# A decoder layer's output projection: the residual added by accumulating transfers, the second norm in rows of its own

## The chip, the cores and the metric

The kernel runs on one core of a Trainium2 chip. The metric is the device time of one execution in microseconds (us), lower is better. The time before is the median of three runs. The profile is that of one further execution, whose own time stands in the table below beside its span.

## The reference

One layer of a decoder with 1024 tokens of 1024 numbers, all in float32. What the change touches is the middle of it:

```
m = concat([rmsnorm(a, attn_group_norm), rmsnorm(c, conv_group_norm)])
x = x + rmsnorm(m @ w_out, mix_post_norm)          # x1
h = rmsnorm(x, ffn_pre_norm)
f = (silu(h @ w_gate) * (h @ w_up)) @ w_down
x = x + rmsnorm(f, ffn_post_norm)
x = x + sigmoid(x @ w_ple_gate) * rmsnorm(p @ w_ple_proj, ple_norm)
```

Ahead of it stand the first norm, the combined input projection, latent attention with 8 heads (`a`) and a gated short convolution (`c`).

## The kernel before, in words

The layer is computed stage after stage: input projection and convolution, attention by heads, output projection, gate and up projections of the feed-forward part, down projection, and the last gate. Every product is split in two: a number is written as a high and a low part (`split`, lines 209 and 210: a cast on ScalarE, a difference on VectorE), and three matmuls take the place of one. The feed-forward products are arranged as seven products of half-size blocks in place of eight (`factor` builds the weight side, `product` does the 12 matmuls of one, lines 1192 to 1195).

Memory is handed out by the program itself. `mf(n)` takes n units of 512 float32 columns from an arena of 30 units, and `free` gives them back; among free places the one that has been free longest is taken. A second argument limits the place: `ML` is units 0 to 22, `MG` 18 to 22, `MW` 0 to 8. Whoever writes into a place waits for the last reader of what was there.

The order of the work on each engine is not quite that of the program. A planner (the Tile scheduler) goes through the program with durations of its own and puts first on an engine what it believes to be ready; each engine and each DMA queue then runs its list strictly in order. All transfers of this stage are issued by SyncE (SP).

The output projection works through eight row tiles t of 128 tokens. The attention half is multiplied here (`wo_half`, 24 matmuls); the convolution half was multiplied earlier, and its rows wait in DRAM as `y_d`. One pass of the loop at the end of the printed code does, for different tiles:

- `wo_a(t)`: 24 matmuls; VectorE adds them, scaled, to the row y loaded from `y_d` (line 1071); `row_norm(t, 0)` takes the mean square on ScalarE (line 230), adds epsilon on VectorE (line 226) and raises to the power -0.5 on GpSimd (line 227).
- `wo_x1(t - 1)`: VectorE multiplies y by the norm and a gain, in place (line 1077), adds the row of x (line 1079), SyncE stores the sum as x1 (line 1081), and `row_norm(t - 1, 1)` takes the second mean square.
- `load_x(t)`: SyncE loads the next row of x (line 1059).
- `wo_n(t - 2)`: VectorE multiplies y by the second norm and gain, in place (line 1086).
- `h2_turn(t - 3)`: TensorE transposes the row (line 1106), ScalarE and VectorE copy it out. The first four tiles are split into `B11` and `B21` and stored raw in `hr_d` (line 1116); the last four go into `tr`, `b12` and `b22` below.
- `load_y(t + 2)` (line 1055) and, near the end, `raw_load` of raw gate and up weights (line 1148).

In the passes after the last tile the first four products of the feed-forward stage run; they need `B11` and `B21` of the first four tiles only. The next eight products (`fp` 1 and 2) need the same and raw weights. Everything after needs sums over all eight tiles (line 1303): `t2` and the splits `T1` to `T4`, of `b12`, `b22` and of `hr_d` read back.

Of the kernel before, what the change touches and what calls it, by code (L numbers as in the profile page):

```python
# [12 lines left out]
ALU = mybir.AluOpType  # L13
AX = mybir.AxisListType

P = 128
# [29 lines left out]
T = S // P  # L46
# [53 lines left out]
def free(*bufs):  # L100
    for b in bufs:
        m = b.arena
        m.clock += 1
        for i in range(b.lo, b.lo + b.n):
            assert m.live[i]
            m.live[i] = False
            m.freed[i] = m.clock
# [28 lines left out]
def hybrid_layer(ctx: ExitStack, tc: tile.TileContext, x, x_t, p_t, cols_in, positions,  # L136
# [3 lines left out]
    act, dve, pe, pool, sp = nc.scalar, nc.vector, nc.tensor, nc.gpsimd, nc.sync  # L140

    x, out = x[0], out[0]
# [10 lines left out]
    mf = Arena(big.tile([P, FU * U], F32, name="mem_f"), FU)  # L153
# [21 lines left out]
    ML, MG, MW = ((0, 22),), ((18, 22),), ((0, 8),)  # L175
# [24 lines left out]
    def cols(n):  # L200
        lo = small_at[0]
        small_at[0] += n
        assert small_at[0] <= 128
        return small[:, lo : lo + n]

    def split(h, l, src, gain=None, eng=None):

        if gain is None:
            act.copy(h, src)  # L209
            (eng or dve).tensor_tensor(l, src, h.bitcast(F32), op=ALU.subtract)  # L210
        else:
            act.mul(h, src, gain)
            dve.scalar_tensor_tensor(l, src, gain, h.bitcast(F32), op0=ALU.mult,
                                     op1=ALU.subtract)
# [20 lines left out]
    def bank3(ap, k):  # L235
        return ap.rearrange("p (k c) -> p k c", k=k)
# [330 lines left out]
    for step in START.split():  # L567
        op, t = step[0], int(step[1:] or 0)
# [412 lines left out]
    ss_y = cols(2 * T)  # L981
# [63 lines left out]
    g_mix, g_ffn = mf(2, MG), mf(2, MG)  # L1045
# [2 lines left out]

    rows_y, rows_x = {}, {}

    def load_y(t):
        rows_y[t] = mf(2, ML)
        sp.dma_start(rows_y[t].a, y_d[t * P : (t + 1) * P, :])

    def load_x(t):
        rows_x[t] = mf(2, ML)
        sp.dma_start(rows_x[t].a, x[t * P : (t + 1) * P, :])

    def row_norm(t, i):
        r = ss_y[:, 2 * t + i : 2 * t + i + 1]
        junk = mr(2, BJ)
        mean_sq(junk.a, rows_y[t].a, D, r)
        free(junk)
        rstd_of(r)

    def wo_a(t):
        y = rows_y[t].a
        ids, b = wo_half(t, mTa, 0)  # L1070
        dve.scalar_tensor_tensor(y, b, ss_a[:, t : t + 1], y, op0=ALU.mult, op1=ALU.add)
        ps.put(ids)
        row_norm(t, 0)

    def wo_x1(t):
        y, xr = rows_y[t].a, rows_x.pop(t)
        dve.scalar_tensor_tensor(y, y, ss_y[:, 2 * t : 2 * t + 1], g_mix.a, op0=ALU.mult,
                                 op1=ALU.mult)
        dve.tensor_tensor(y, y, xr.a, op=ALU.add)
        free(xr)  # L1080
        sp.dma_start(x1_d[t * P : (t + 1) * P, :], y)
        row_norm(t, 1)

    def wo_n(t):
        y = rows_y[t].a
        dve.scalar_tensor_tensor(y, y, ss_y[:, 2 * t + 1 : 2 * t + 2], g_ffn.a, op0=ALU.mult,
                                 op1=ALU.mult)

# [2 lines left out]
    def four(b):  # L1093
        return b.a.rearrange("p (k c) -> p k c", k=4)

    def h2_turn(t):
        src = rows_y.pop(t)
        o = slice(t % 4 * P, (t % 4 + 1) * P)
        first = t < T // 2
        if first:  # L1100
            raw = mf(2, ML)
        for q in range(2):
            ids, b = ps.get()
            for j in range(4):
                k = 4 * q + j
                pe.transpose(b[:, j * P : (j + 1) * P], src.a[:, k * P : (k + 1) * P], ident[:])
            if first:
                act.copy(raw.a[:, q * U : (q + 1) * U], b)
            else:
                act.copy(four(tr[q])[:, :, o], bank3(b, 4))  # L1110
            if first or q:
                h, l = tf["B" + "12"[q] + "12"[not first]]
                split(four(h)[:, :, o], four(l)[:, :, o], bank3(b, 4))
            ps.put(ids)
        if first:
            sp.dma_start(hr_d[:, :, o], raw.a.rearrange("p (k c) -> p k c", k=KD))
            free(raw)
        free(src)
# [12 lines left out]
    def pair(n, where):  # L1131
        return mr(n, where), mr(n, where)
# [11 lines left out]
    def raw_load(fp, i, where=None):  # L1144

        for m, w in enumerate((w_gate, w_up)):
            raws[fp, m, i] = r = mf(2, where)
            sp.dma_start(r.a, w[2 * fp + i])

    def factor(fp, m, p):  # L1150
        eng = pool if fp else dve
        a = raws[fp, m, 0].a
        a11, a12 = a[:, 0:U], a[:, U:]
        if p == 1:
            src = a11
        elif p == 2:
            src = a12
        else:
            b = raws[fp, m, 1].a
            a21, a22 = b[:, 0:U], b[:, U:]  # L1160
            if p == 6:
                eng.tensor_tensor(a21, a21, a22, op=ALU.add)
                eng.tensor_tensor(a11, a21, a11, op=ALU.subtract)
                src = a11
            elif p == 5:
                src = a21
            elif p == 7:
                eng.tensor_tensor(a21, a22, a11, op=ALU.subtract)
                src = a21
            elif p == 3:  # L1170
                eng.tensor_tensor(a12, a12, a11, op=ALU.subtract)
                src = a12
            else:
                src = a22
        h, l = wp[fp, m, p] = pair(1, RR)
        split(h.a, l.a, src)
        if p == ORDER[-1]:
            free(raws.pop((fp, m, 0)), raws.pop((fp, m, 1)))
# [75 lines left out]
    for t in range(T + 3):  # L1254
        if t < T:
            wo_a(t)
        elif t == T:
            for d in (mTa, wo):
                for h, l in d.values():
                    free(h, l)  # L1260
            for i in head[:2]:
                product(*i)
        elif t == T + 1:
            for i in head[2:]:
                product(*i)
        if 1 <= t <= T:
            wo_x1(t - 1)
        if t < T:
            load_x(t)
        if 2 <= t <= T + 1:  # L1270
            wo_n(t - 2)
        if t == T + 1:
            free(g_mix, g_ffn)
            t2 = mf(4, MG)
            tf["T1"], tf["T4"] = pair(4, BT), pair(4, BT)
            b11, b21 = tf["T1"][1].a.bitcast(F32), tf["T4"][1].a.bitcast(F32)
            sp.dma_start(b11.rearrange("p (k c) -> p k c", k=4), hr_d[:, 0:4, :])
            sp.dma_start(b21.rearrange("p (k c) -> p k c", k=4), hr_d[:, 4:8, :])
        if t >= 3:
            h2_turn(t - 3)  # L1280
        if t + 2 < T:
            load_y(t + 2)
        if t == T - 1:
            raw_load(0, 1, ML)
        if t == T:
            raw_load(1, 0, ML)
        if t == T // 2:
            for i in head:
                factor(*i)
    b12, b22 = tr[0], tr[1]  # L1290

    def both(f, fp, p):
# [239 lines left out]
    for i in range(n2):  # L1532
# [17 lines left out]
        if j in tail:  # L1550
            f, t = tail[j]
# [66 lines left out]
```

## Time and profile before

| | |
|---|---|
| median of three runs | 1226.24 us (1225.47 to 1227.34) |
| the profiled execution's own time | 1227.49 us |
| its span, first to last instruction | 1225.4 us |
| mean granted TensorE clock | 0.99 |
| busy: TensorE, VectorE, ScalarE, GpSimd | 98%, 66%, 48%, 41% |
| output projection's tiles and the change's reach | about 438 to 531 us of the span |

In the rows of the profile, PE is TensorE (PEld its weight loads), DVE VectorE, ACT ScalarE, POOL GpSimd, SP SyncE; L1071 is line 1071 of the code. A row of the timeline gives start, duration, engine, line, operation, what it writes and reads, and in brackets how long the engine was idle before and what ended that. A row of the waits gives who waited, for whom, the total, how often, and the longest.

### The profile page before, as it was taken

The page shows a single profiled execution, that of the slowest core. Times are in us where ns is not written, and L with a number is a line of the kernel's source. Part 1 is how long each engine was busy: PE and PEld are TensorE (multiplying, and loading weights), DVE is VectorE, ACT ScalarE, POOL GpSimd, SP SyncE. Part 2 cuts the span into 40 slices and gives each one's busy share as a digit, 9 for nine tenths or more (in the row PEclk, how much of TensorE's full clock was granted, in tenths as well). Part 3 has the DMA queues.
Part 4 walks back from the last instruction along what each step waited for, and adds up shares of the span by engine and source line. Part 5 has one row for each costly group of instructions (what it writes and reads, how often), then busy time and mean ns, then how long its engine had stood idle before and what let it go on. Part 6 is the DMA issues. An engine that isn't in the chain of part 4 may idle for free.

```text
span 1225.4 us, 16706 instructions
## 1 busy us (share of the span) xinstructions
PE 1201.5 (98%) x5918; PEld 1012.2 (83%) x5918; DVE 810.6 (66%) x1173; ACT 587.3 (48%) x1079; POOL 503.8 (41%) x392
## 2 busy tenths in 40 slices
PE   8999999999999999789999999999999999999998
PEld 6998888889999888678788888888888888888886
DVE  6676346478867758785657665565556677758775
ACT  7543333267766736543433333333345546545652
POOL 4433534226554311025888646674634102202321
PEclk8999999999999999889999999999999999999999
DMA  8712553994561667524465445543566576654342
GB/s 267 258 39 104 184 202 133 278 365 90 135 161 44 232 223 252 203 104 143 161 229 197 140 144 190 178 157 118 209 209 200 184 242 230 233 172 164 120 136 79
DMA packets 89821, 217.77 MB, mean 178 GB/s; under 512 B 9030, under 2 KB 18026, under 8 KB 88426
## 3 DMA queue, kind: packets, MB, share of 16 engines
q1 hardware_dynamic: 89392, 216.17, 53.4%
q8 instruction: 46, 0.75, 0.3%
q10 hardware_dynamic: 346, 0.54, 0.2%
q14 instruction: 37, 0.30, 0.1%
HBM read 145.38 MB, written 71.04 MB: 177 GB/s over the span
## 4 chain that ended last, share of the span: by engine, by line
PE 80%; DVE 6%; DMA 5%; issue 3%; ACT 3%; POOL 2%; ACTq 0%; POOLq 0%; DVEq 0%; SPq 0%
PE banks L1192 10%; PE banks L1195 10%; PE banks L1194 10%; PE banks L220 7%; PE banks L222 7%; PE banks L221 7%; PE banks L1391 6%; PE banks L1390 6%; PE banks L1389 6%; PE banks L894 2%; DVE mem_r L210 2%; PE banks L1498 1%; PE banks L1501 1%; PE banks L1500 1%; PE banks L865 1%
## 5 line engine op out<-in xcount | busy, mean ns | idle before, releaser
L210 DVE TENSOR_TENSOR mem_r<-mem_f,mem_r 128x512 fp32r<-128x512 f32 (+1 forms) x404 | 374.4, 958 | 206.4 <-ACT mem_r L209 194.1
L209 ACT CAST mem_r<-mem_f 128x512 fp32r<-128x512 f32 (+2 forms) x407 | 258.4, 666 | 410.6 <-PE banks L1194 128.7
L1192 PE MATMUL banks<-mem_r 128*128 128x512 f32 x616 | 242.0, 393 | 4.5 <-ACT mem_r L209 3.4
L1194 PE MATMUL banks<-mem_r 128*128 128x512 f32 x616 | 241.6, 392 | 0.0
L1195 PE MATMUL banks<-mem_r 128*128 128x512 f32 x616 | 240.8, 392 | 0.1
L220 PE MATMUL banks<-mem_r 128*128 128x512 f32 (+2 forms) x536 | 196.3, 371 | 2.4 <-ACT mem_r L209 1.7
L221 PE MATMUL banks<-mem_r 128*128 128x512 f32 (+2 forms) x536 | 196.4, 368 | 1.3 <-POOL mem_r L210 1.2
L222 PE MATMUL banks<-mem_r 128*128 128x512 f32 (+2 forms) x536 | 196.0, 368 | 0.0
L1192 PEld LDWEIGHTS banks<-mem_r 128*128 128x128 f32 x616 | 116.5, 189 | 30.7 <-ACT mem_r L209 5.0
L1195 PEld LDWEIGHTS banks<-mem_r 128*128 128x128 f32 x616 | 116.7, 189 | 25.7 <-DVE mem_r L210 1.1
L1194 PEld LDWEIGHTS banks<-mem_r 128*128 128x128 f32 x616 | 116.8, 190 | 24.3 <-DVE mem_r L210 0.2
L1391 PE MATMUL banks<-mem_r 128*128 128x512 f32 x308 | 119.8, 389 | 0.0
L1390 PE MATMUL banks<-mem_r 128*128 128x512 f32 x308 | 119.8, 389 | 0.0
L1389 PE MATMUL banks<-mem_r 128*128 128x512 f32 x308 | 119.8, 390 | 0.0
L220 PEld LDWEIGHTS banks<-mem_r 128*128 128x128 f32 x536 | 101.2, 190 | 19.1 <-ACT mem_r L209 2.8
L221 PEld LDWEIGHTS banks<-mem_r 128*128 128x128 f32 x536 | 101.6, 190 | 17.4 <-POOL mem_r L210 1.4
L222 PEld LDWEIGHTS banks<-mem_r 128*128 128x128 f32 x536 | 101.5, 189 | 16.1
L879 POOL TENSOR_TENSOR mem_f<-mem_f,stats 128x640 f32<-128x640 f32 (+5 forms) x64 | 73.4, 1161 | 92.0 <-DVE stats L878 49.4
L227 POOL TENSOR_TENSOR small<-small,mhalf 128x1 f32<-128x1 f32 (+2 forms) x46 | 37.6, 821 | 177.5 <-DVE small L226 177.0
L1210 DVE TENSOR_TENSOR mem_f<-banks,mem_f 128x512 f32<-128x512 f32 x66 | 45.2, 686 | 55.9 <-PE banks L1195 55.8
L210 DVE TENSOR_TENSOR mem_r<-banks,mem_r 128x512 fp32r<-128x512 f32 (+3 forms) x118 | 69.3, 612 | 12.9 <-ACT mem_r L209 12.3
L1390 PEld LDWEIGHTS banks<-mem_r 128*128 128x128 f32 x308 | 57.8, 188 | 12.0
(197 smaller groups left out, 1890.0 us busy)
## 6 DMA issues: line engine op xcount, KB each, us to landing
sc_d<-mem_f SPq DMA_DIRECT2D x77, 256.0 KB, 3.5
mem_f<-sc_d SPq DMA_DIRECT2D x77, 256.0 KB, 3.0
mem_f<-in_w_gate_dram SPq DMA_DIRECT2D x22, 512.0 KB, 5.2
mem_f<-in_w_up_dram SPq DMA_DIRECT2D x22, 512.0 KB, 5.1
mem_f<-in_w_down_dram SPq DMA_DIRECT2D x22, 512.0 KB, 4.5
wc_d<-mem_f SPq DMA_DIRECT2D x22, 512.0 KB, 2.7
mem_f<-wc_d SPq DMA_DIRECT2D x44, 256.0 KB, 3.1
mem_f<-in_w_down_dram SPq DMA_DIRECT2D x33, 256.0 KB, 3.4
```

The costliest lines, as they stand in the source:

```text
L209: act.copy(h, src)
L210: (eng or dve).tensor_tensor(l, src, h.bitcast(F32), op=ALU.subtract)
L220: pe.matmul(o, wh, vh, start=i == 0, stop=False)
L221: pe.matmul(o, wh, vl, start=False, stop=False)
L222: pe.matmul(o, wl, vh, start=False, stop=i == n - 1)
L879: pool.tensor_tensor(pt.a[:, 0:n], pt.a[:, 0:n], sm.to_broadcast([P, n]), op=ALU.mult)
L1192: pe.matmul(b, wh.a[:, c], th[:, k], start=first and k == 0, stop=False, skip_group_check=True)
L1194: pe.matmul(b, wh.a[:, c], tl[:, k], start=False, stop=False, skip_group_check=True)
L1195: pe.matmul(b, wl.a[:, c], th[:, k], start=False, stop=k == 3, skip_group_check=True)
L1389: pe.matmul(b, ah.a[:, c], bh.a, start=first, stop=False, skip_group_check=True)
L1390: pe.matmul(b, ah.a[:, c], bl.a, start=False, stop=False, skip_group_check=True)
L1391: pe.matmul(b, al.a[:, c], bh.a, start=False, stop=last, skip_group_check=True)
```

## The change

The row of x is no longer loaded into a buffer and added by VectorE. A transfer on the GpSimd queue reads it from DRAM and adds it to y in memory (`accum_op`). The x1 store and the second mean square follow that transfer. The second norm writes into new rows (`rows_n`), and y is freed there. y is loaded one tile later than before in program order, the two raw weight loads of the loop may use units 0 to 18 only, the two gains are freed at separate points, and `t2` is taken after the loop.

```
-    rows_y, rows_x = {}, {}
+    rows_y = {}
...
-    def load_x(t):
-        rows_x[t] = mf(2, ML)
-        sp.dma_start(rows_x[t].a, x[t * P : (t + 1) * P, :])
...
     def wo_x1(t):
-        y, xr = rows_y[t].a, rows_x.pop(t)
+        y = rows_y[t].a
         dve.scalar_tensor_tensor(y, y, ss_y[:, 2 * t : 2 * t + 1], g_mix.a, op0=ALU.mult,
                                  op1=ALU.mult)
-        dve.tensor_tensor(y, y, xr.a, op=ALU.add)
-        free(xr)
+        pool.dma_start(y, x[t * P : (t + 1) * P, :], accum_op=ALU.add)
         sp.dma_start(x1_d[t * P : (t + 1) * P, :], y)
         row_norm(t, 1)
 
+    rows_n = {}
+
     def wo_n(t):
-        y = rows_y[t].a
-        dve.scalar_tensor_tensor(y, y, ss_y[:, 2 * t + 1 : 2 * t + 2], g_ffn.a, op0=ALU.mult,
-                                 op1=ALU.mult)
+        y = rows_y.pop(t)
+        rows_n[t] = mf(2, ML)
+        dve.scalar_tensor_tensor(rows_n[t].a, y.a, ss_y[:, 2 * t + 1 : 2 * t + 2], g_ffn.a,
+                                 op0=ALU.mult, op1=ALU.mult)
+        free(y)
...
     def h2_turn(t):
-        src = rows_y.pop(t)
+        src = rows_n.pop(t)
...
-        if t < T:
-            load_x(t)
+        if t == T:
+            free(g_mix)
         if 2 <= t <= T + 1:
             wo_n(t - 2)
         if t == T + 1:
-            free(g_mix, g_ffn)
-            t2 = mf(4, MG)
+            free(g_ffn)
...
-        if t + 2 < T:
-            load_y(t + 2)
+        if 1 <= t < T - 1:
+            load_y(t + 1)
         if t == T - 1:
-            raw_load(0, 1, ML)
+            raw_load(0, 1, ((0, 18),))
         if t == T:
-            raw_load(1, 0, ML)
+            raw_load(1, 0, ((0, 18),))
...
+    t2 = mf(4, MG)
```

## The prediction

> **What bounds the kernel now.** I read the page first, then the busy time by stretches around the output projection, what TensorE waited for there, and last the order of VectorE, ScalarE and SyncE in the same stretch.
>
> ```profile
> span 1225.4 us, 16706 instructions
> PE 1201.5 (98%) x5918; PEld 1012.2 (83%) x5918; DVE 810.6 (66%) x1173; ACT 587.3 (48%) x1079; POOL 503.8 (41%) x392
> ```
>
> TensorE is busy for 98% of the span, so whatever another engine saves counts only where TensorE stands still. The changed stage is one such place (columns: stretch, its length, busy time and count of PE, PEld, DVE, ACT, POOL, then the granted clock, the DMA share, GB/s):
>
> ```profile
> 444.00:484.00 40.00, 40.00 (x195) 33.47 (x194) 33.12 (x41) 21.02 (x40) 7.90 (x11) 1.00 0.72 237
> 484.00:498.00 14.00, 13.75 (x67) 10.82 (x65) 12.99 (x20) 9.57 (x17) 2.48 (x4) 1.00 0.74 245
> 498.00:531.00 33.00, 22.45 (x81) 17.58 (x82) 26.68 (x27) 16.25 (x24) 0.93 (x1) 0.74 0.43 156
> 531.00:560.00 29.00, 28.94 (x126) 23.28 (x125) 20.96 (x20) 11.97 (x21) 12.43 (x9) 1.00 0.37 127
> ```
>
> TensorE runs through 444 to 498 without a gap, loses 33.00 - 22.45 = 10.55 us idle between 498 and 531, and is full again after that. In the same stretch the granted clock is 0.74, so of the 22.45 busy microseconds 22.45 x 0.26 = 5.8 are slow clock. At most 10.55 + 5.8 = 16.4 us can be won here. The two gaps and what ended them:
>
> ```profile
> PE banks L1106 <- issue: 7.3, 1, 7.3
> PE banks L1192 <- ACT mem_r L209: 3.4, 2, 3.1
> 484.45 0.73 PE L1192 MATMUL banks<-mem_r 128*128 128x512 f32 x2
> 505.09 1.94 PE L1106 MATMUL banks<-ident,mem_f 128*128 128x128 f32 x8 [7.34 <-issue]
> 507.37 0.79 PE L1192 MATMUL banks<-mem_r 128*128 128x512 f32 x1 [0.34 <-ACT mem_r L209]
> 525.31 0.79 PE L1192 MATMUL banks<-mem_r 128*128 128x512 f32 x1 [3.09 <-ACT mem_r L209]
> 525.90 0.63 PE L1194 MATMUL banks<-mem_r 128*128 128x512 f32 x1
> 526.33 0.63 PE L1195 MATMUL banks<-mem_r 128*128 128x512 f32 x1
> 531.57 0.40 PE L1194 MATMUL banks<-mem_r 128*128 128x512 f32 x1
> 531.80 0.40 PE L1195 MATMUL banks<-mem_r 128*128 128x512 f32 x1
> ```
>
> The projection's last matmul is over at 484.45, where the first products of the next stage begin. The first gap ends with row tile 6's transposes (L1106), the second with a split of late weights (L209). After a gap matmuls start 0.43 us apart (525.90 to 526.33) and only about six microseconds later 0.23 apart (531.57 to 531.80).
>
> Why the transposes are late is VectorE's order:
>
> ```profile
> 448.43 1.28 DVE L1071 SCALAR_TENSOR_TENSOR mem_f<-banks,small,mem_f 128x1024 f32<-128x1024 f32 x1
> 451.76 1.29 DVE L1077 SCALAR_TENSOR_TENSOR mem_f<-mem_f,small 128x1024 f32<-128x1024 f32 x1 [0.67 <-POOL small L227]
> 479.83 1.28 DVE L1071 SCALAR_TENSOR_TENSOR mem_f<-banks,small,mem_f 128x1024 f32<-128x1024 f32 x1 [0.48 <-DMA mem_f<-y_d]
> 490.61 1.27 DVE L1071 SCALAR_TENSOR_TENSOR mem_f<-banks,small,mem_f 128x1024 f32<-128x1024 f32 x1
> 496.71 1.22 DVE L1079 TENSOR_TENSOR mem_f<-mem_f 128x1024 f32<-128x1024 f32 x1
> 503.71 1.28 DVE L1086 SCALAR_TENSOR_TENSOR mem_f<-mem_f,small 128x1024 f32<-128x1024 f32 x1 [4.39 <-DMA x_d<-mem_f]
> 508.56 1.28 DVE L1086 SCALAR_TENSOR_TENSOR mem_f<-mem_f,small 128x1024 f32<-128x1024 f32 x1
> 511.78 1.03 PE L1106 MATMUL banks<-ident,mem_f 128*128 128x128 f32 x8
> ```
>
> Row 6's second norm (503.71) writes in place over y, so it waited 4.39 us for the x1 store that reads y. Row 7's norm follows at 508.56, its transposes end at 512.8. Row 7 was late before that: TensorE had it ready at 484.4, but its sum with y began at 490.61. SyncE tells why:
>
> ```profile
> 486.03 0.32 SPq L1055 DMA_DIRECT2D mem_f<-y_d  x1
> 493.09 0.33 SPq L1059 DMA_DIRECT2D mem_f<-in_x_dram  x1
> 498.33 0.49 SPq L1148 DMA_DIRECT2D mem_f<-in_w_gate_dram  x1
> 521.18 0.33 SPq L1148 DMA_DIRECT2D mem_f<-in_w_up_dram  x1
> SPq L1055 <- DMA hr_d<-mem_f: 10.6, 3, 5.8
> SPq L1059 <- DMA hr_d<-mem_f: 6.1, 1, 6.1
> ```
>
> The seven two-unit slots that 22 units leave beside four for raw weights and four for gains hold y, x and the transposed rows. Three y loads and one x load waited for an hr_d store to leave a slot (10.6 and 6.1 us), row 7's y and x among them, and SyncE stood behind them.
>
> **The change part by part.** *The sums go.* Eight L1079 sums of 1.22 leave VectorE. Off the path that is nothing; on it, in 484 to 498, where VectorE is busy 12.99 of 14.00, it lets row 7's steps start when their inputs are there.
>
> *The accumulate comes.* Eight transfers on the GpSimd queue, each behind its L1077 and ahead of the x1 store and the second mean square. No row shows one. The nearest are plain 512 KB transfers, median issue to landing, the first two lines from 444 to 484, the others from 484 to 510:
>
> ```profile
> x_d<-mem_f SPq DMA_DIRECT2D x6, 512.0 KB, 2.9
> mem_f<-in_x_dram SPq DMA_DIRECT2D x4, 512.0 KB, 4.8
> x_d<-mem_f SPq DMA_DIRECT2D x2, 512.0 KB, 9.4
> mem_f<-in_w_up_dram SPq DMA_DIRECT2D x2, 512.0 KB, 10.8
> 451.17 0.56 POOL L227 TENSOR_TENSOR small<-small,mhalf 128x1 f32<-128x1 f32 x1 [4.14 <-DVE small L226]
> 453.19 1.52 POOL L227 TENSOR_TENSOR small<-small,mhalf 128x1 f32<-128x1 f32 x1 [1.46 <-DVE small L226]
> ```
>
> So L, from the end of L1077 to landing, lies between 2.9 and 10.8; it cannot be below zero, since a transfer must follow the norm. I take 6: x's own load, 4.8, plus 1.2 for GpSimd's issue, between the 0.56 and 1.52 of its other instructions. The same row reaches memory as before, so the total of bytes loaded stays.
>
> A rule of the Trainium skill speaks against it. Here DMA runs at 0.72 to 0.74 of its time over 444 to 498, at some 240 GB/s. The Trainium skill's "Collectives: The Full Stack", section "The bandwidth ceiling: the fold count and why AG ≠ RS ≠ AR", says that an add inside the DMA path needs two source reads and halves the rate. No run here shows it yet; by it, L would be nearer 10, row 7 four microseconds later, the gain some 4 us smaller, 1220.6 in place of 1216.6.
>
> *Row 7's chain.* From the start of L1071 to L1077 an unhindered row takes 451.76 - 448.43 = 3.33 (square, add, power between). New chain: sum at 484.5, L1077 at 487.8, done 489.1, landed 489.1 + L, second norm's square, add and power 3.33 - 1.28 = 2.05, L1086 1.28, transposes about 1.0: end at 493.4 + L, so 499.4 with L = 6 and 504.2 with 10.8, against 512.8. The x1 store is off this path, since L1086 writes rows of its own (same 1.28).
>
> *Queues.* On GpSimd the issue waits for L1077; behind it stands the next row's power, some 1.5 us at worst, and VectorE waits for that. It is covered by a row's TensorE time, 24 matmuls x 0.23 + 1.0 = 6.5 us. On SyncE the x1 store now waits for the accumulate, and y(t+1), which the program now asks for one row later, may stand behind it. Its slot is free rows earlier, so the planner can issue it first. If not, a row may start only 4.61 (L1071 to the end of L1077) + L + 0.3 issue + 4.8 load = 15.7 after the one two before it, in place of 13: 1.35 us a row, seven rows, 9.5 us, and the tail stands at 508.9, still before 512.8. The eight x issues leave SyncE.
>
> *Slots and weights.* Tracing the allocator by hand through the old loop gives the waits above: y(5), y(6), y(7) and x(7) in the slots of hr_d stores, and the gate weights (1,0) in x(7)'s, issued at 498.33, just after x(7)'s sum ended at 497.93. The same tracing for the new loop puts y(4) to y(7) in slots that the second norm or the transposes gave up rows before, gate (1,0) in y(6)'s and up (1,0) in the fifth norm row's. y(6)'s slot is free when row 6's second norm has read it and its x1 store has landed: 479.83 + 4.61 + 6 = 490.4 for the accumulate, and 2.9 to 9.4 for the store, so 493.3 to 499.8 (the norm is done at 493.8). With 4.8 to 10.8 for the load and 1.3 for split and cast, gate (1,0) is usable between 499.9 and 511.9, middle 506. Up (2,0) still takes b12's slot, as it did at 521.18, 8.4 after the last transposes; it moves with them to 507.8.
>
> *The sum.* TensorE has its first four products until 498, as before, then two tiles of transposes (2 us), and if the planner puts the up weights first, 2.7 us of their products (12 matmuls x 0.23): until 502. Waiting until 506 leaves one gap of 4 us. The slow clock behind it costs what it cost at 525, 14 matmuls x 0.2 = 2.8. Left over is 6.8 of 16.4; the gain is 9.6 us. All else (the gains freed earlier, t2 after the loop) issues no instruction and is taken at nothing; it has the full TensorE after 531 to hide in. The profiled execution took 1227.49 (span 1225.4 and 2.1 around it), 1.25 over the median of 1226.24: 1217.9 for it, 1216.6 for the median.
>
> On the re-warming the row differs from a page: from 525.31 the slow matmuls last until about 531. The Trainium skill's "TensorE: Matmul & The Clock Gate", section "What's actually happening", gives 3.4 us of sustained work for it; by that the gap would cost 1.7, not 2.8, and the time be 1215.5.
>
> **The rivals.** *No change: the weights were the wait.* At 507.37 the first product came 0.34 us after the transposes, released by a split, so weights loaded from 498.33 were about as late. If gate (1,0) is again issued near 498 and lands as slowly, only the 1.94 us of transposes move into the gap: 1224.3. For it: DMA is crowded with hr_d, x1 and weights at the tail. Against it: y(6)'s slot comes free up to 5 us earlier, and half of the weights do not wait for it.
>
> *Slower: ScalarE waits for the transfer with the next row behind it.* ScalarE works in order. If a row's second square stands ahead of the next row's first, the row period is L1077 1.28 + L + two squares 2.5 + add and power 0.8 = L + 4.6 against TensorE's 6.5. Over seven rows the tail ends at 493.4 + L + 7 (L - 1.9) = 480.1 + 8L: later than 512.8 from L = 4.1 on. At 4.8 it is 518.5, 5.7 later, 1231.9; at 6 it is 528.1, 15.3 later, 1241.5. Against it:
>
> ```profile
> 449.75 1.06 ACT L230 ACTIVATE mem_r<-mem_f 128x1024 fp32r<-128x1024 f32 x1 [3.54 <-DVE mem_f L1071]
> 450.88 1.06 ACT L230 ACTIVATE mem_r<-mem_f 128x1024 fp32r<-128x1024 f32 x1
> ```
>
> The square at 449.75 is row 1's first (it follows the L1071 of 448.43); row 0's second comes behind it, at 450.88. With two rows in flight the period is (L + 4.6) / 2, harmless until L = 8.4. For it: the planner orders by its own durations, and none of its guesses for an accumulate is visible here.
>
> *The accumulate is far dearer.* With L above 493.4 + L = 512.8, 19.4 us, the tail would be as late as now; no transfer of this size in the rows took that long. It counts as part of the slower case.
>
> **How the numbers follow.** The forecast has 0.62, no change 0.15, slower 0.23. Its own bounds are 1209.8 (all 16.4 won) and 1222.5 (gate weights at 511.9 in place of 506: 5.9 less gained). The range 1209.8 to 1231.9 takes in the no-change case and the near end of the slower one; what it leaves out is the far half of that case, 0.12, and little below. A measurement of this kernel tells about 0.2%, 2.5 us, from no change. Faster by more than that: 0.62 + 0.02 of the no-change case, 0.64; within: 0.13; slower: 0.23.
>
> **What would show it.** Right: no x loads on SyncE, eight accumulates landing in about 6 us, L1071 of row 7 within a microsecond or two of 484.5, its transposes over near 500, no wait of L1086 for an x1 store, TensorE's idle time after 498 at about 4 us, at one place, behind weights. Wrong: second squares that hold up ScalarE row after row, y loads behind x1 stores, idle time of TensorE before 498, or accumulates of 10 us and more.

## The result, and the profile after

The changed kernel takes 1234.65 us, the median of five executions, against 1226.24 before (1225.47 to 1227.48). Four of the five lie between 1231.76 and 1236.88; the fifth, of 3653.29, and one of e8 below, of 2434.99, are left out of the ratios. The ratio is 1.0063 with a 95% interval of 1.0043 to 1.0083: slower by about 8 us, where 9.6 us less was forecast. The profiled execution took 1234.65 as well, with a span of 1232.9, 7.5 over the span before.

The lines of the page that answer to those of before:

```profile
span 1232.9 us, 16712 instructions
PE 1201.0 (97%) x5918; PEld 1011.2 (82%) x5918; DVE 804.9 (65%) x1165; ACT 587.8 (48%) x1079; POOL 512.9 (42%) x400
```

Eight sums have left VectorE and eight issues have come to GpSimd. TensorE's busy time is the same, so the time went where TensorE stands still or runs slowly. Busy time by stretches, in the prediction's columns:

```profile
444.00:484.00 40.00, 37.47 (x178) 30.24 (x178) 22.78 (x30) 15.84 (x29) 10.39 (x16) 1.00 0.77 196
484.00:498.00 14.00, 10.39 (x38) 7.93 (x37) 11.09 (x16) 9.65 (x20) 3.60 (x5) 0.76 0.96 253
498.00:531.00 33.00, 23.53 (x107) 19.25 (x106) 22.37 (x26) 18.20 (x28) 3.50 (x4) 0.84 0.64 204
531.00:560.00 29.00, 27.06 (x113) 20.45 (x111) 26.87 (x24) 14.97 (x22) 11.37 (x7) 1.00 0.31 110
```

Idle time is 2.53 + 3.61 + 9.47 + 1.94 = 17.55 us, against 0.25 + 10.55 + 0.06 = 10.86 before. Slow clock costs 10.39 x 0.24 + 23.53 x 0.16 = 6.3, against 5.8. Together 23.8 against 16.7: 7.2 of the 7.5 us lie in these stretches. The 10.55 us after 498 have become 9.47, so little was won there; new are 6.1 us of idle time before 498, where TensorE stood for only 0.25.

The waits that grew are those for the new transfer (columns: waiter, releaser, sum of us, times, longest):

```profile
ACT mem_r L230 <- DMA mem_f<-in_x_dram: 16.1, 5, 6.0
PE banks L1192 <- ACT mem_r L209: 10.3, 3, 8.7
SPq L1077 <- DMA mem_f<-in_x_dram: 31.3, 6, 13.0
ACT mem_f L1108 <- DMA hr_d<-mem_f: 5.8, 3, 2.4
```

ScalarE stands five times, 16.1 us in all, in front of a second mean square (L230) whose row is still being accumulated: rows 0, 1, 2, 6 and 7. In rows 3 to 5 the landing is over before the square's turn comes; there the copies of a transposed row (L1108) stand ahead of it, and they wait three times, 5.8 us in all, for a store of `hr_d` to leave their slot. The accumulates themselves, by the view of their line, are about as long as forecast in the median:

```profile
L1076 POOL DMA_DIRECT2D mem_f<-in_x_dram x8: 884/886/1068, 447.7 to 505.7; - x8
DMA to landing us min/median/max: 5.4/5.8/10.0
```

How a wait on one engine reaches TensorE is seen at rows 2 and 4, on the timelines of VectorE, GpSimd, SyncE, ScalarE, VectorE and TensorE, in this order (start, duration, instruction, idle time before it and its releaser):

```profile
458.17 1.28 DVE L1074 SCALAR_TENSOR_TENSOR mem_f<-mem_f,small 128x1024 f32<-128x1024 f32 x1 [0.66 <-POOL small L227]
...
460.01 0.89 POOL L1076 DMA_DIRECT2D mem_f<-in_x_dram  x1 [1.88 <-DVE small L226]
...
470.37 0.59 SPq L1116 DMA_DIRECT2D hr_d<-mem_f  x1
...
470.07 1.06 ACT L230 ACTIVATE mem_r<-mem_f 128x1024 fp32r<-128x1024 f32 x1 [5.96 <-DMA mem_f<-in_x_dram]
...
471.25 0.15 DVE L226 TENSOR_SCALAR small<-small 128x1 f32<-128x1 f32 x1 [5.24 <-ACT mem_r L230]
471.33 1.28 DVE L1067 SCALAR_TENSOR_TENSOR mem_f<-banks,small,mem_f 128x1024 f32<-128x1024 f32 x1
...
472.67 0.50 PE L220 MATMUL banks<-mem_r 128*128 128x512 f32 x1 [1.73 <-DVE mem_f L1067]
```

Row 2's accumulate is issued at 460.01 and lands at 470.0. ScalarE waits 5.96 for it, VectorE waits 5.24 for ScalarE, and right behind stands row 4's sum (L1067), which empties TensorE's banks: TensorE waits 1.73 for that. All three engines work in order, so one late landing holds row 4, whose own inputs were there. It also holds SyncE: row 2's x1 store goes out at 470.00, and only behind it, at 470.37, the first `hr_d` store, for which the later copies then wait. From L1074 of row 2 to that of row 4 (474.70, below) 16.5 us pass.

While row 2's accumulate was on its way the DMA engines had hardly a free moment. The same ten microseconds in the changed kernel, then in e1 below, which has the same instructions without the add:

```profile
460.00:470.00 10.00, 10.00 (x53) 8.48 (x52) 4.76 (x6) 3.09 (x6) 2.91 (x4) 1.00 0.99 247
460.00:470.00 10.00, 10.00 (x51) 8.40 (x50) 6.99 (x10) 4.65 (x11) 2.79 (x5) 1.00 0.87 291
```

They were busy for 0.99 of the time and moved less, 247 GB/s against 291.

The same loop from row 4 to row 6, where the landing is no longer what the square waits for, on VectorE, GpSimd, SyncE, ScalarE and VectorE again:

```profile
474.70 1.28 DVE L1074 SCALAR_TENSOR_TENSOR mem_f<-mem_f,small 128x1024 f32<-128x1024 f32 x1 [0.66 <-POOL small L227]
...
476.28 0.88 POOL L1076 DMA_DIRECT2D mem_f<-in_x_dram  x1 [1.62 <-DVE mem_f L1074]
...
481.95 0.32 SPq L1077 DMA_DIRECT2D x_d<-mem_f  x1
...
483.55 0.59 ACT L1108 COPY mem_f<-banks 128x512 f32<-128x512 f32 x1 [2.45 <-DMA hr_d<-mem_f]
...
485.47 1.09 ACT L230 ACTIVATE mem_r<-mem_f 128x1024 fp32r<-128x1024 f32 x1
...
486.76 1.28 DVE L1067 SCALAR_TENSOR_TENSOR mem_f<-banks,small,mem_f 128x1024 f32<-128x1024 f32 x1
490.07 1.28 DVE L1074 SCALAR_TENSOR_TENSOR mem_f<-mem_f,small 128x1024 f32<-128x1024 f32 x1 [0.66 <-POOL small L227]
```

From L1074 of row 4 to its issue 1.58; to the landing, marked by the x1 store that waited for it, 5.67; to the second square 3.52, because a transposed row's copies stand ahead on ScalarE and waited 2.45 for a store to leave their slot; to row 6's sum 1.29; to row 6's L1074 3.31. That is 15.37 us for two rows, 7.7 a row, where TensorE needs 6.5. In e1, without the add, the same loop takes 15.8 (467.60 to 483.38): what the changed kernel loses against e1 it has lost by row 4.

The tail, on the same timelines; the landing is that of the load at 502.50 alone:

```profile
494.87 1.28 DVE L1067 SCALAR_TENSOR_TENSOR mem_f<-banks,small,mem_f 128x1024 f32<-128x1024 f32 x1
...
503.19 0.69 DVE L1162 TENSOR_TENSOR mem_f<-mem_f 128x512 f32<-128x512 f32 x1 [4.58 <-DMA mem_f<-in_w_gate_dram]
503.86 1.27 DVE L1074 SCALAR_TENSOR_TENSOR mem_f<-mem_f,small 128x1024 f32<-128x1024 f32 x1
...
505.69 0.88 POOL L1076 DMA_DIRECT2D mem_f<-in_x_dram  x1 [0.15 <-issue]
...
502.50 0.33 SPq L1148 DMA_DIRECT2D mem_f<-in_w_up_dram  x1
DMA to landing us min/median/max: 11.4/11.4/11.4
...
514.21 1.06 ACT L230 ACTIVATE mem_r<-mem_f 128x1024 fp32r<-128x1024 f32 x1 [4.93 <-DMA mem_f<-in_x_dram]
...
516.21 2.19 ACT L209 CAST mem_r<-mem_f 128x512 fp32r<-128x512 f32 x4
...
516.89 0.79 PE L1192 MATMUL banks<-mem_r 128*128 128x512 f32 x1 [8.74 <-ACT mem_r L209]
```

Row 7's sum, forecast for 484.5, begins at 494.87. Its L1074 stands behind a weight's sum (L1162) that waits for a load. Its accumulate lands at 514.2. TensorE waits 8.74 us for the casts of weights that begin at 516.21. The first pair of the four is of the up weights: in e1, which has the same order, the pair behind it waits for the gate weights. The up weights, issued at 502.50, landed at 513.9. From then until 516.21, 2.3 us, ScalarE was held by row 7's second square, which waited for the accumulate, and by a transposed row.

### The profile page after: what moved, and what is told of

Same layout as the page of the kernel before. It is cut to its first block, busy times and chain, and to the rows that moved or that the text cites. A ratio compares the mean times of both kernels' runs of the same rounds, so it can differ in the third digit from the quotient of the medians.

```text
span 1232.9 us, 16712 instructions
## 1 busy us (share of the span) xinstructions
PE 1201.0 (97%) x5918; PEld 1011.2 (82%) x5918; DVE 804.9 (65%) x1165; ACT 587.8 (48%) x1079; POOL 512.9 (42%) x400
## 3 DMA queue, kind: packets, MB, share of 16 engines
q0 software_dynamic: 1152, 4.19, 2.0%
## 4 chain that ended last, share of the span: by engine, by line
PE 83%; DMA 6%; DVE 5%; ACT 2%; issue 2%; POOL 1%; SPq 0%; DVEq 0%; ACTq 0%; POOLq 0%
PE banks L1195 11%; PE banks L1194 11%; PE banks L1192 11%; PE banks L220 7%; PE banks L221 7%; PE banks L222 7%; PE banks L1390 6%; PE banks L1389 6%; PE banks L1391 6%; PE banks L894 2%; DMA mem_f<-in_x_dram 2%; DVE mem_r L210 2%; DMA hr_d<-mem_f 1%; PE banks L1501 1%; PE banks L1498 1%
```

## The experiments

Medians are given with the ratio to the kernel before and its 95% interval. The kernel before had medians of 1225.47 to 1226.79 beside them. An edit is shown against the changed kernel, or against the run that its heading names; `...` stands for lines left out. e1, e9, e10 and e13 to e15 leave out all or part of the sum with y, so their results are not those of the layer.

### The transfer without its add, more slots, the rows alone, the accumulate alone

**e1: the same transfer, without the add.**

```diff
-        pool.dma_start(y, x[t * P : (t + 1) * P, :], accum_op=ALU.add)
+        pool.dma_start(y, x[t * P : (t + 1) * P, :])
```

> The GpSimd transfer writes x's row over y in place of adding it, in the same place and order; this leaves the residual sum out. Theory A (the add inside the transfer is what costs: by the traces 1152 packets of 4.19 MB took 25.5% of 95 us of the DMA engines, the other 17.67 MB 54.9%, so about twice the time per byte): landing falls from 5.4 to 10.0 us towards 4 to 5, the row that took 10.0 us loses its delay, and the time falls by 3 to 6 us, to 1229 to 1231. Theory B (the four raw copies of the transposed rows share one slot, so each waits for the hr_d store before it): the stores still land 5 to 6.5 us after issue and the time stays within 2 us of 1234.7.

Measured: 1226.65, ratio 1.001 (0.9998 to 1.0021). Every engine has the same instructions in the same order as in the changed kernel; only the add is gone, and with it 8.0 us by the medians (6.5 by the two ratios, 0.0053 of 1226), more than its theory A gave the add. Landing, waits and the four stretches:

```profile
DMA to landing us min/median/max: 3.8/4.5/7.9
```

```profile
PE banks L1192 <- ACT mem_r L209: 10.0, 3, 8.2
...
ACT mem_r L230 <- DMA mem_f<-in_x_dram: 7.3, 3, 4.4
```

```profile
444.00:484.00 40.00, 40.00 (x198) 33.40 (x196) 27.49 (x36) 19.18 (x36) 10.29 (x18) 1.00 0.73 241
484.00:498.00 14.00, 12.40 (x57) 9.68 (x56) 10.20 (x16) 10.55 (x19) 4.15 (x5) 1.00 0.85 277
498.00:531.00 33.00, 23.70 (x101) 19.04 (x102) 27.47 (x27) 18.80 (x26) 0.56 (x1) 0.84 0.39 140
531.00:560.00 29.00, 27.93 (x120) 21.57 (x119) 24.94 (x26) 12.47 (x22) 15.74 (x10) 1.00 0.37 127
```

Up to 498 TensorE idles 1.60 us, not 6.1, and ScalarE's wait has fallen from 16.1 to 7.3. The gap at the tail, 8.2 us behind casts, has stayed. So what the add costs shows before 498, and the tail's gap is there without it. The up weights' load, issued at 494.01, and the casts on ScalarE show what that gap waits for:

```profile
DMA to landing us min/median/max: 12.6/12.6/12.6
507.23 1.15 ACT L209 CAST mem_r<-mem_f 128x512 fp32r<-128x512 f32 x2
509.44 1.14 ACT L209 CAST mem_r<-mem_f 128x512 fp32r<-128x512 f32 x2 [1.06 <-DMA mem_f<-in_w_gate_dram]
```

The up weights landed at 506.6, their casts began at 507.23, and TensorE went on at 507.91.

**e2: two slots for the transposed rows**, so that ScalarE's copies do not wait for a store.

```diff
+            if raw_was:
+                free(raw_was.pop())
...
-            free(raw)
+            raw_was.append(raw)
```

> The changed kernel with each raw copy of a transposed row held until the next one has its place, so that two slots alternate. Theory B: ScalarE's three waits for hr_d stores (5.8 us) are gone, the row period of rows 4 to 7 falls from 8.1 us towards TensorE's 6.5, row 7's sum with y moves from 494.9 to about 489, and the time falls by 4 to 8 us, to 1227 to 1231. Theory A: the accumulates, which the chain of waits goes through for 28% of the stage, keep the period, and the time stays within 2 us of 1234.7.

Measured: 1235.95, ratio 1.0089 (1.0072 to 1.0105). The waits for the store are gone, but the wait in front of the second squares grew and the median landing is 7.6:

```profile
ACT mem_r L230 <- DMA mem_f<-in_x_dram: 20.3, 6, 4.4
```

So taking away the copies' waits wins nothing: without them ScalarE waits for the accumulates instead.

**e3: the rows alone.** The x loads and VectorE's sums are put back; the second norm keeps its own rows, and y its later load.

```diff
-        pool.dma_start(y, x[t * P : (t + 1) * P, :], accum_op=ALU.add)
+        xr = rows_x.pop(t)
+        dve.tensor_tensor(y, y, xr.a, op=ALU.add)
+        free(xr)
...
+        if t < T:
+            load_x(t)
```

> The second norm in rows of its own, the slots and weight loads of the changed kernel, but x's rows loaded into buffers by SyncE and added by VectorE as before. Theory A: without the accumulate the loss of 8.4 us is gone; about as before or faster, 1220 to 1228. Theory C (new rows, later y loads and new places of the weights are what costs, whoever adds x): slower than before by 4 us or more, 1230 to 1235.

Measured: 1222.99, ratio 0.9982 (0.9971 to 0.9993): the lowest median of the study, 0.2% below the kernel before (0.07 to 0.29% by the interval). Its profiled execution shows:

```profile
484.00:498.00 14.00, 9.68 (x38) 7.62 (x39) 11.55 (x17) 8.61 (x18) 1.59 (x3) 0.88 0.77 264
498.00:531.00 33.00, 30.14 (x131) 23.84 (x130) 32.08 (x33) 23.07 (x32) 0.55 (x1) 0.95 0.39 145
```

After 498 the idle time falls from 10.55 to 2.86 us, but 4.32 come before it.

**e4: the kernel before with the accumulate alone**: the second norm in place, y loaded two rows ahead, the weights as before.

```diff
-        dve.tensor_tensor(y, y, xr.a, op=ALU.add)
-        free(xr)
+        pool.dma_start(y, x[t * P : (t + 1) * P, :], accum_op=ALU.add)
...
-        if t < T:
-            load_x(t)
```

> The kernel before with the accumulating transfers alone: second norm in place, y loaded two tiles ahead, weights as before. Theory A: slower than before by 5 to 12 us, 1231 to 1238 (the norm now waits for accumulate and store both). Theory C: within 3 us of before, 1223 to 1229. Theory B: hr_d stores alternate over slots here, so nearer to before than the changed kernel, 1226 to 1231.

Measured: 1240.85, ratio 1.0129 (1.0109 to 1.0148), above all three expectations. Here the norm waits for the x1 store again, and the store for the accumulate:

```profile
DVE mem_f L1085 <- DMA x_d<-mem_f: 8.7, 3, 3.4
```

The two parts of the change thus point in opposite directions: the accumulate alone loses 14.5 us, the rest without it wins 3.4 (2.2 by the ratio). That rest is the rows together with the later y load and the new places of the weights; e12 below takes the later y load out of it.

### What else could make the difference

**e5: the tail's first weights kept out of the hr_d slot**, where they waited and held up row 7's norm (L1162 ahead of L1074 above); `hr_at` notes where those slots lay.

```diff
-            raw_load(0, 1, ((0, 18),))
+            raw_load(0, 1, ((0, hr_at[-1]), (hr_at[-1] + 2, 18)))
```

> The changed kernel with the raw weights (0,1) kept out of the slot of the last hr_d store. In the changed kernel VectorE stood 4.58 us at 503.19 before their factor, with row 7's post-norm multiply (503.86) behind it. Theory A1 (the add's longer transfers cost twice: in the row loop and, through the queues, in row 7's tail): the wait in the tail is separate and shrinks, row 7's multiply comes about 3.3 us after its sum in place of 9.0, and the time falls by 3 to 6 us, to 1229 to 1232. Theory A2 (only the row loop counts, the tail has other work in front of TensorE): within 2 us of 1234.7.

Measured: 1234.2, ratio 1.0067 (1.0047 to 1.0086). Row 7's L1074 now comes 4.4 us after its sum instead of 9.0, and the time is the same: ScalarE's casts at the tail now wait for the load of the up weights itself.

```profile
514.81 1.14 ACT L209 CAST mem_r<-mem_f 128x512 fp32r<-128x512 f32 x2 [0.25 <-DMA mem_f<-in_w_up_dram]
```

**e6: e3 with a second store of each row on the GpSimd queue**, which nothing waits for: the load on the DMA without the wait.

```diff
         sp.dma_start(x1_d[t * P : (t + 1) * P, :], y)
+        pool.dma_start(x1b_d[t * P : (t + 1) * P, :], y)
```

> The rows-only kernel (1222.99) with a second store of x1 on the GpSimd queue to a place that nobody reads: about 1.8 us of all DMA engines more per row (18.1% of 80 us for eight plain 512 KB transfers on that queue), which is a little more than the add took over a plain load, but nothing waits for its landing except the reuse of a slot. Theory D (DMA engine time as such): slower than rows-only by 4 us or more, 1227 to 1232. Theory E (the landing that the row chain waits for): within 2.5 us of rows-only, 1221 to 1225.5.

Measured: 1226.55, ratio 1.0006 (0.9993 to 1.002), 3.6 over e3. The program was ordered anew for it, so part of this can be the order; it lies between what the two theories expected.

**e7: e3 with the accumulate in row tiles 0 to 3 only**; the edit is against the changed kernel.

```diff
-        pool.dma_start(y, x[t * P : (t + 1) * P, :], accum_op=ALU.add)
+        if t < T // 2:
+            pool.dma_start(y, x[t * P : (t + 1) * P, :], accum_op=ALU.add)
+        else:
+            xr = rows_x.pop(t)
+            dve.tensor_tensor(y, y, xr.a, op=ALU.add)
+            free(xr)
...
+        if T // 2 <= t < T:
+            load_x(t)
```

> The rows-only kernel with the accumulate for tiles 0 to 3 alone; tiles 4 to 7 load x and add on VectorE. The whole accumulate cost 1234.65 - 1222.99 = 11.7 us over rows-only. If the loss is made row by row in the loop (theory A2), about half of it is left, 1227 to 1230. If it is made in row 7's tail (theory A1), nearly all of it is gone, 1222 to 1225.5.

Measured: 1227.83, ratio 1.0013 (1.0 to 1.0026): 4.8 of the 11.7 us between e3 and the changed kernel.

**e8: e3 with e2's two slots.**

> The rows-only kernel with two alternating slots for the raw copies, a try for a version better than both. Its SyncE waits 9.3 us in four pieces for hr_d stores before x loads. If those waits hold up the tail, 1219 to 1222; if they are covered, within 2 us of 1222.99.

Measured: 1226.35, ratio 1.0 (0.9985 to 1.0015), 3.4 over e3, where a gain or no change was expected. The slots are no gain there either.

**e12: e3 with y loaded two rows ahead, as before.**

```diff
-        if 1 <= t < T - 1:
-            load_y(t + 1)
+        if t + 2 < T:
+            load_y(t + 2)
```

> The rows-only kernel (1222.99) with y loaded two tiles ahead in program order, as in the kernel before; a try for a version better than both. In rows-only row 5's sum waited 1.25 us for its y. If late y rows hold up the tail, 1219 to 1222; if they are covered, within 2 us of 1222.99; if the seventh slot is then missing for x, as in the kernel before, 1224 to 1227.

Measured: 1224.75, ratio 0.9999 (0.9988 to 1.001), not better than e3: the later y load costs nothing. By this ratio the rows with y loaded as before win nothing either, so e3's gain belongs, if to anything, to the rows and the later y load together.

### The add: its landing or its load, a few rows or all

**e9: e1 with three quarters of each row stored once more** by SyncE: more load in place of the add.

```diff
         sp.dma_start(x1_d[t * P : (t + 1) * P, :], y)
+        sp.dma_start(x1b_d[t * P : (t + 1) * P, 0:768], y[:, 0:768])
```

> The plain-write kernel of the first experiment (1226.65; the sum with y is left out) with 384 KB more stored per row by SyncE behind the x1 store, to a place nobody reads: about 1.1 us of all DMA engines per row, what the add took over a plain transfer on the GpSimd queue (3.0 against 1.8 us). No row waits for it. Theory D (the add's DMA engine time delays all other transfers): 1231 to 1235. Theory E (the landing that the rows wait for): 1225 to 1229.

Measured: 1228.54, ratio 1.0016 (1.0002 to 1.0029), 1.9 over e1. This is not load alone: x's rows landed later too, in 6.3 in the median, more than the accumulates' 5.8, but none took over 7.5. So a median landing of six is not in itself what costs.

**e10: e1 in two halves that overlap by a column**, so that the second must follow the first: a later landing in place of the add.

```diff
-        pool.dma_start(y, x[t * P : (t + 1) * P, :])
+        pool.dma_start(y[:, 0:U], x[t * P : (t + 1) * P, 0:U])
+        pool.dma_start(y[:, U - 1 :], x[t * P : (t + 1) * P, U - 1 :])
```

> The plain-write kernel with its transfer in two halves of 512 and 513 columns that share one column, so that GpSimd issues the second only when the first has landed: about the same bytes and DMA time, but the row is complete some 7 us after the first issue in place of 4.5 (the sum with y is left out). The planner sees the two steps and orders the engines for them. Theory E1 (a later landing costs, planned or not): 1230 to 1236. Theory E2 (it costs only where the order of the engines does not reckon with it): 1225 to 1229. Theory D: no change of DMA time, so 1225 to 1229.

Measured: 1233.59, ratio 1.0057 (1.0042 to 1.0072), 6.9 over e1, with no add in it. The engines' time on this queue is as in e1 (17.8% of 440 to 520, against 18.1%); what grew is ScalarE's wait, nearly to that of the changed kernel:

```profile
ACT mem_r L230 <- DMA mem_f<-in_x_dram: 15.0, 4, 5.9
```

**e11: the accumulate in two independent halves**, for a shorter landing.

```diff
-        pool.dma_start(y, x[t * P : (t + 1) * P, :], accum_op=ALU.add)
+        for c in (slice(0, U), slice(U, D)):
+            pool.dma_start(y[:, c], x[t * P : (t + 1) * P, c], accum_op=ALU.add)
```

> The changed kernel with each accumulate in two independent halves of 512 columns, 256 KB each. The add and its DMA time stay, and the planner orders the engines for two transfers. Theory D: 1232 to 1237, as the changed kernel. Theory E2: with an order that reckons with a longer step, 1227 to 1232.

Measured: 1237.09, ratio 1.0085 (1.007 to 1.0101). A half lands in 6.4 in the median, later than a whole row did (5.8).

**e13, e14, e15: the add in row tiles 0 to 3, in 4 to 7, in tile 2 alone**, and the plain write of e1 in the others; the order of the instructions is that of the changed kernel.

```diff
-        pool.dma_start(y, x[t * P : (t + 1) * P, :], accum_op=ALU.add)
+        pool.dma_start(y, x[t * P : (t + 1) * P, :], **(dict(accum_op=ALU.add) if t < 4 else {}))
```

> Instruction order of the changed kernel on every engine; tiles 0 to 3 are accumulated, tiles 4 to 7 overwritten by x without the add. Theory F (a few unlucky landings in the row loop set it: in the changed kernel row 4's sum came at 471.33, in the plain-write kernel at 464.23, 7.1 us earlier, and the distance stayed near that): 1232 to 1235. Theory G (every accumulate adds its share): half of 8 us, 1229.5 to 1231.5.

> The same order; tiles 4 to 7 are accumulated, tiles 0 to 3 overwritten without the add. Theory F: the rows of the loop stay early and only the last accumulate shows, 1226.5 to 1229. Theory G: half of 8 us, 1229.5 to 1231.5.

> The same order; tile 2 alone is accumulated. Theory F: its 10.0 us from issue to landing cost about 5 us of the 8, 1230 to 1233. Theory G: an eighth of 8 us, 1226 to 1229.

Measured: 1231.6, ratio 1.0044 (1.0027 to 1.006); 1230.95, ratio 1.0038 (1.0024 to 1.0052); 1227.91, ratio 1.0011 (0.9999 to 1.0024). Over e1 that is 5.0, 4.3 and 1.3 us. The halves add up to 9.3, the whole is 8.0: both halves cost. Row 4's sum comes at 464.23 in e1, 464.60 in e14, 470.86 in e13 and 471.33 in the changed kernel, so each half's loss arises in its own rows. That the long landing of row 2 makes the whole difference has fallen by e14, which loses 4.3 us without it. For the first half it has not fallen: row 2 landed after 9.6 us in e13, and after only 6.0 in e15, so e15 does not try a long landing at all. Nor does it measure what a single add costs, since its interval holds e1's ratio.

## Why the prediction was wrong

**Two misses.** The result is 18.0 us over the forecast, and e1 parts this: without the add, with the same instructions in the same order, the kernel takes 1226.65, still 10.0 over the forecast of 1216.6. The add brings the other 8.0. So two steps failed, one in the rows and one at the tail.

**The step that failed in the rows** is "With two rows in flight the period is (L + 4.6) / 2, harmless until L = 8.4", taken with one L of 6 for all eight rows. Two rows were in flight, as argued from the squares at 449.75 and 450.88. The loop that a landing closes, from L1074 of row 2 to that of row 4, took 16.5 us. Of these, 10.6 lie between the end of the norm (458.17 + 1.28) and the landing, and 6.0 are the rest. The formula's 4.6 left out row 4's own sum of 1.28, which stands on VectorE behind row 2's epsilon. So by this loop the limit is 13.0 - 6.0 = 7.0, not 8.4. The forecast's 6 is under both limits, row 2's 10.6 is over both. Row 3's sum had come 1.7 us later than in e1 (459.64 against 457.90), row 4's came 7.1 later and row 7's 6.7 (494.87 against 488.21): the rows behind never made it up. Nor had the forecast a place for the second way of the wait, by SyncE: x1 stores that wait for accumulates hold up the `hr_d` stores behind them, and these the copies on ScalarE.

**L itself** was well sized as a median: 6 forecast from the end of the norm, and 5.97 in row 4 (474.70 + 1.28 to 481.95). But from its issue a landing took 10.0 in row 2 and 8.5 in row 7 (505.69 to 514.2), against a median of 5.8, and one long landing was enough to set the loop back. The prediction's own bounds went up to 10.8, and it named accumulates of 10 us among the signs of being wrong.

**The rival** "ScalarE waits for the transfer with the next row behind it" was right in its mechanism and was given 0.23, because the limit lay too high and one L stood for all. That the result lies within its price, 1231.9 to 1241.5, is luck in part: it was reckoned with one row in flight and a delay in every row, and neither was so.

**The step that failed at the tail** is "Waiting until 506 leaves one gap of 4 us". (By its own terms the sum is 498 + 2 + 2.7 = 502.7, not 502, and the gap 3.3.) It counted on the up weights being there and on the gate weights being the wait. What TensorE waited for were casts of the up weights, in the changed kernel and without the add: they landed 11.4 and 12.6 us after their issue, at 513.9 and 506.6, and the gaps are 8.74 and 8.18. Of the 8.74 at most 2.3 are the order on ScalarE, where row 7's second square stands ahead of the casts; in e1 it is 0.6. In e5 the casts wait for that load directly. In e1 TensorE's idle time in the four stretches is 12.0 us and the slow clock costs 23.70 x 0.16 = 3.8; the forecast left 6.8 for both together. The rival "No change: the weights were the wait" was right that weights are the wait, and its 1224.3 is 2.3 under e1. But the weights that it named, the gate weights of 498.33, took 10.4 us to land, until 508.7, which is after the release at 507.37: in the kernel before, too, the wait was for the up weights.

**Row 7's chain** began at 494.87, not 484.5, since its sum stood behind the loop of the rows before; its L1074 came 9.0 us after the sum, not 3.3. The forecast took the start from TensorE, not from the loop. Even in e1 it is 488.21.

**The Trainium skill's "Collectives: The Full Stack"**, section "The bandwidth ceiling: the fold count and why AG ≠ RS ≠ AR", was weighed too lightly. Packets, MB and share of the 16 engines' time on the GpSimd queue between 440 and 520, the changed kernel first, then e1:

```profile
q0 software_dynamic: 1152, 4.19, 30.2%
q0 software_dynamic: 1152, 4.19, 18.1%
```

The same 4.19 MB take 30.2% with the add and 18.1% without: 3.0 and 1.8 us of all engines a row, a factor of 1.67. The page's rule, half the rate, stated there for a ReduceScatter, is nearly borne out for the engines' time. For the median landing it is not, which rose by 1.3 us (4.5 to 5.8), while row 2's went from 4.5 to 10.0. The estimate of 1220.6 moved the forecast the right way, but its 4 us are half of what the add cost, because it counted one row's delay and not the loop's.

**Right** were the parts around it. The in-place norm's wait for the x1 store is gone, and the x loads left SyncE. No run shows a gain from VectorE's lighter load. The rows of their own with the later y load gain 3.4 us in e3, not 9.6, and part of the idle time only moves ahead of 498; with y loaded as before (e12) no gain is clear of noise.

**The whole, by medians:** the rows and what came with them -3.4 (e3), x's transfer moved onto the chain behind the norm +3.7 (e1 against e3, which differ in the order of their instructions too), the add in it +8.0: 1234.65. By the ratios the three are -2.2, +3.4 and +6.5.

**What stays open** is how the add's cost divides between its later landing and its time on the DMA engines. e10 (a later landing without more load, 6.9) speaks for the landing, e9 (more load and a somewhat later landing, 1.9) against a cost of the load as such. But both were ordered anew, and neither imitates one side exactly; and in the changed kernel the two go together, since row 2's long landing falls where the DMA engines were busy for 0.99 of the time. What made the load of the up weights take 11 to 13 us was not tried either. How the planner's order would look with a dearer price for an accumulate was not tried.

## What to carry to other kernels

As this case shows, a sum on an engine with time to spare is not worth replacing by a transfer, if the transfer then stands between two steps of a chain that in-order engines share with the next rows: before, x was loaded ahead of need, and only the 1.2 us sum was on the chain; after, 5.8 us of landing were. When a rival turns on a loop's period, write out the whole loop, from one row's instruction to the same instruction of the row that waits for it, with all that is queued in between on each engine, and compare that with the bound engine's time for a row. Put in the longest landing that the rows allow, not only the usual one: here one of 10 us set the next row but one back by more than 5. Test the parts of a change alone: here, taking away the add alone showed that less than half of the miss was the add's, and that the forecast gain was not there even without it.

## What the runs showed of the hardware

An accumulating transfer of 512 KB on the GpSimd queue occupies the DMA engines 1.67 times as long as the plain one. The same bytes by SyncE's queue cost about 1.6 us, worked out from the trace of before between 440 and 520:

```profile
q1 hardware_dynamic: 8443, 18.01, 67.0%
```

67.0% of 80 us for 18.01 MB is 1.56 us for 0.524 MB, half of the accumulate's 3.0.

Issuing one holds GpSimd for 0.88 us, and split in halves it lands no sooner: a half took 6.4 in the median in e11, a whole row 5.8.

After the tail's gap TensorE was slow for some 3.9 us, from 516.89 to where matmuls start 0.24 apart, against 5.7 after 525.31 before; behind the gap that ended at 492.18 it was some 4.7 (0.23 apart from 496.89 on):

```profile
520.76 0.40 PE L1194 MATMUL banks<-mem_r 128*128 128x512 f32 x1
521.00 0.40 PE L1192 MATMUL banks<-mem_r 128*128 128x512 f32 x1
```

So the 3.4 us of the Trainium skill's "TensorE: Matmul & The Clock Gate", section "What's actually happening", are nearer to this gap than to that one; with transposes among the first matmuls here, the two are not quite alike.
